# Splitting each raw weight tile into high and low parts in one operation per engine

## The chip, the cores and the metric

The kernel runs on one core of a Trainium2 chip. The metric is the device time in microseconds (us) of one execution, given as the median of several runs. The engines are TensorE (PE in the profile; its weight loads are listed as PEld), VectorE (DVE), ScalarE (ACT), GpSimd (POOL) and SyncE (SP), whose queue issues nearly all DMAs.

## The reference, cut to what matters

A decoder trunk of two layers in float32, with 256 tokens and 2048 channels. Nearly all of its arithmetic is products of the activations with weight matrices, and every one of these products that the change touches is computed to float32 accuracy.

```
# layer 0 (state space)
h  = modulate(rmsnorm(x, norm_g[0]), shift, scale)    # from c @ mod_w[0]
u, z = split(h @ w_in)                                # 2048 x 4096
y  = gelu(s5_scan(u))                                 # recurrence over tokens
y  = y * sigmoid(y @ w_glu + b_glu)
x  = x + gate * ((y * silu(z)) @ w_out)
# shared keys and values
kv = modulate(rmsnorm(x, kv_norm_g), ...) @ w_kv      # 2048 x 3072
# layer 1 (attention with three branches)
q, gates, z = split(h @ w_qg)                         # 2048 x (2048 + 48 + 6144)
o  = sum over branches of gates * silu(z) * attention(branch)
x  = x + gate * (o @ w_o)
return rmsnorm(x, final_norm_g)
```

The vectors shift, scale and gate come from products of one row, silu(c), with the matrices mod_w (2048 x 6144 for each layer) and kv_mod_w (2048 x 4096). All weights are read once.

## The kernel before

Activations lie with channels on the 128 partitions, as 16 blocks of [128, 256 tokens]. A weight matrix is cut into columns of 128, and each such column into two raw tiles of [128, 8, 128] float32, 512 KB each, which is 1024 columns on a partition. TensorE multiplies float32 numbers fast if they are first rounded to a shorter form (fp32r). So each weight tile and each activation is split: the high part is the rounded value, the low part is what is left. A product is then the sum of three: high x high, high x low, low x high (lines 227 to 229).

Raw tiles land in `ring`, a pool of 8 slots that all weights share: the split weights, those of the adaLN products that TensorE computes as they lie (`pe_mod_pair`, lines 155 and 157), and those that VectorE multiplies and sums (`dve_mod`, lines 142 and 144). One DMA on SP's queue fills one slot, and it is issued when what used the slot before has finished.

`split_w` (lines 194 to 205) cuts a raw tile of eight blocks into two halves of four blocks, 512 columns. For each half ScalarE writes the high part (line 202) and then VectorE subtracts it from the raw tile (line 203). The results lie in `hring`, a pool with 4 buffers of [128, 4, 128] for high parts and 4 for low parts. `project_half` (lines 222 to 229) consumes one raw tile with 24 matmuls: for each of eight blocks high x high, high x low, low x high. A high buffer is free after the last matmul of line 228 that reads it, a low buffer after the last of line 229.

The stages, in order of the profile: the adaLN products of layer 0 together with eight blocks of u, row by row of w_in (`u_rows`), to some 150 us; the tables of the state space layer and its scan, a recurrence of small VectorE operations (lines 608 to 611), with the blocks of u and z as filling, to some 410 us; the products with w_glu and w_out, to some 610 us; keys and values, compression and queries (four blocks of these row by row, `q_rows`, with raw tiles of 512 columns), to some 900 us; attention head by head with the 48 blocks of its z, to some 1260 us; the product with w_o and the last norm. A list written out by hand (`PLAN`) says at which point of the program the filling work stands: halves of u and z, adaLN products of TensorE and of VectorE, pieces of the compression and rows of the queries. The order of the instructions of each engine is then set when the program is built: the framework orders them by a timeline that it simulates, with the buffers that the pools have (`schedule_with_timeline_sim=True`). On the chip each engine and each DMA queue works in that order.

Of the kernel before, what the change touches and what calls it, by code (L numbers as in the profile page):

```python
# [37 lines left out]
# columns of the adaLN products, by blocks of 128: 0..47 layer 0, 48..95 layer 1, 96..127 keys and values.  # L38
# Blocks 0..31 come first; of the rest TensorE takes some (weights as they lie) and VectorE the others (turned round).
# [16 lines left out]
SK = 2  # L56
# what fills each slot of the program: u, z halves of blocks, m, d modulation (TensorE, VectorE),
# c pieces of the compression, q rows of the queries
# [12 lines left out]
def trunk_kernel(ctx, tc, xT, crow, ccol, vec, m0n, mn, mt, w_ur, w_in, w_glu, w_out, w_kv, w_qr, w_q, w_g,  # L71
# [3 lines left out]
    ring = ctx.enter_context(tc.tile_pool(name="ring", bufs=8))  # L75
    hring = ctx.enter_context(tc.tile_pool(name="hring", bufs=4))
# [16 lines left out]
    def raw_tile(name="raw"):  # L93
        return ring.tile([128, 8, 128], F32, tag="raw", name=name)

    # ---------------------------------------------------------------- constants
# [78 lines left out]
    # columns of modv: 0..47 layer 0, 48..95 layer 1, 96..127 kv  # L175
    def mod_finish(col, n):
        """Those of the columns col .. col + n that VectorE has summed, in two parts."""
        t = [x for x in range(col, col + n) if x in DVE_MODS]
        if t:
            c = slice(t[0], t[-1] + 1)  # L180
            assert len(t) == t[-1] + 1 - t[0]
            nc.vector.tensor_add(modv[:, c], modv[:, c], modw[:, c.start - 48:c.stop - 48])
            nc.vector.tensor_add(modv[:, c], modv[:, c], vv_("mb", c.start, c.stop))

    # ---------------------------------------------------------------- projections
# [8 lines left out]
    def split_w(r, n):  # L194
        """The first n of the eight blocks in r, four by four."""
        out = []
        for h in range(0, n, 4):
            c = min(4, n - h)
            hi = hring.tile([128, 4, 128], F32R, tag="hi", name="hi")
            lo = hring.tile([128, 4, 128], F32R, tag="lo", name="lo")  # L200
            rr = r[:, h:h + c, :]
            nc.scalar.activation(hi[:, 0:c, :], rr, AF.Copy)  # L202
            nc.vector.tensor_sub(lo[:, 0:c, :], rr, hi[:, 0:c, :].bitcast(F32))  # L203
            out.append((hi, lo))
        return out

    class Act:
        """A matrix [2048 channels, 256 tokens] as a high and a low part."""
# [13 lines left out]
    def project_half(src, act, half, acc):  # L222
        w = load_w(src, (half,))
        for k in range(8 * half, 8 * half + 8):
            hi, lo = w[(k - 8 * half) // 4]
            kk = k % 4
# [4 lines left out]
    def project(src, act):  # L231
        """The sums [128 columns, 256 tokens]."""
# [13 lines left out]
    def rms_scale(tot):  # L246
        """1 / sqrt(mean square over channels), for every token, on all partitions."""
# [7 lines left out]
    def norm_mod(xt, rstd, scol, bcol, act, ks=range(KT)):  # L255
        """act = split of (x * rstd) * S + B."""
# [7 lines left out]
    # ---------------------------------------------------------------- layer 0: modulation and u  # L264
    # (the first NR blocks of u, row by row of w_in as the modulation of the rows comes in)
# [14 lines left out]
    def u_rows(k):  # L280
# [6 lines left out]
        for i in range(NR):  # L287
            hi, lo = w[i // 4]
            acc = uacc[i // 2][:, i % 2, :]
            nc.tensor.matmul(acc, hi[:, i % 4, :], h0(0, k), start=(k == 0 and i % 2 == 0), stop=False,  # L290
                             skip_group_check=True)
            nc.tensor.matmul(acc, hi[:, i % 4, :], h0(1, k), start=False, stop=False, skip_group_check=True)
            nc.tensor.matmul(acc, lo[:, i % 4, :], h0(0, k), start=False, stop=(k == KT - 1),
# [10 lines left out]
    # ---------------------------------------------------------------- S5 tables  # L304
# [10 lines left out]
    def exact_exp(dst, src):  # L315
        """e^src to float32's accuracy: 2^k times a polynomial of what is left."""
# [40 lines left out]
    # powers a^1..a^4: [128, 64, 4] real, imaginary  # L357
# [20 lines left out]
    # coef  # L378
# [6 lines left out]
    # coef * a^(3-j): [128, 64, 4]  # L385
# [13 lines left out]
    # a^4 for the chunk recurrence  # L399
# [41 lines left out]
    for s in (2, 3, 0, 1):  # L441
# [11 lines left out]
        # C a^0 .. C a^3 side by side  # L453
# [5 lines left out]
        # K_d[c_in, c_out] = Re(C a^d Bbar) of the pairs (h = (l, q), b) at partitions (q, b, c_in)  # L459
# [16 lines left out]
        # the input tables turned round, in place: (b, j, c) on partitions, [h, r, g2, n]  # L476
# [30 lines left out]
    def u_turn(f):  # L507
        """Half of u, (g, e, c) on partitions, to (e, j, c) on partitions."""
# [53 lines left out]
    def scan_in(f):  # L562
        """Inputs of the recurrence over chunks."""
# [38 lines left out]
    def scan_run(f):  # L602
        """The recurrence over chunks."""
# [9 lines left out]
    def scan_local(f, tz):  # L613
        """What comes out of a chunk from its own inputs, in place of U."""
# [14 lines left out]
    def scan_out(f, cts):  # L629
        """The part of y that the states carry, on to U."""  # L630
        VH = VV[f]
        ys = VH[:, 0:8].rearrange("p h r b k -> p (h r b k)").rearrange("p (b g k) -> p b g k", g=4, k=64)
        for q in range(2):
# [10 lines left out]
            for g2 in range(2):  # L644
# [3 lines left out]
                else:  # L648
                    # VectorE is at the recurrence of the other half
# [53 lines left out]
    # ---------------------------------------------------------------- GLU  # L703
# [30 lines left out]
    # ---------------------------------------------------------------- shared keys and values  # L734
# [46 lines left out]
    def cmp_piece(e, i):  # L781
        """A quarter of the first product of a compression, then the rest of it."""
# [6 lines left out]
        for l in range(8 * half, 8 * half + 8):  # L789
            hi, lo = w[l // 4 - 2 * half]  # L790
            first, last = (h == 0 and l == 0), (h == 1 and l == 15)
            nc.tensor.matmul(cp, hi[:, l % 4, :], f[:, 0, l, :], start=first, stop=False)
            nc.tensor.matmul(cp, hi[:, l % 4, :], f[:, 1, l, :], start=False, stop=False)
            nc.tensor.matmul(cp, lo[:, l % 4, :], f[:, 0, l, :], start=False, stop=last)
# [44 lines left out]
    # (queries of the first heads, row by row of their weights as the modulation of the rows comes in)  # L839
# [3 lines left out]
    def q_rows():  # L843
# [21 lines left out]
        for i in range(QN):  # L865
            hi, lo = w[i // 4]
            acc = qacc[i // 2][:, i % 2, :]
            nc.tensor.matmul(acc, hi[:, i % 4, :], hq[0](0, k), start=(k == 0 and i % 2 == 0), stop=False,
# [254 lines left out]
```

## Time and profile before

| | |
|---|---|
| median of 3 runs | 1364.43 us (1359.98 to 1368.99) |
| span of the profiled execution | 1368.1 us |
| TensorE matmul busy | 1267.0 us, 93% |
| VectorE busy | 1068.3 us, 78% |
| ScalarE busy | 681.7 us, 50% |
| read from HBM | 326.10 MB, 242 GB/s over the span |
| split operations on full raw tiles of 1024 columns, two each | 640 on ScalarE, 640 on VectorE |

The profile is one execution, taken by the hardware profiler; its times stand against its own span, which lies 3.7 us above the median of the runs. An engine's busy time is the time in which one of its instructions ran; a duration reaches to the end of an instruction's writes, so that the next one of the same engine can start a little before it. A wait names the engine that waited, and what released it. In a list of DMAs the last number is the time from issue to landing.

### The profile page before, as it was taken

How to read it: one execution, taken by the hardware profiler on the slowest of the kernel's cores; microseconds unless marked ns; L12 is line 12 of the kernel's file. 1: busy time of each engine (PE TensorE's matmuls, PEld its weight loads, DVE VectorE, ACT ScalarE, POOL GpSimd, SP SyncE). 2: the span in 40 equal slices, each digit the busy share in tenths (PEclk: the TensorE clock that was granted, in tenths of full speed). 3: DMA queues.
4: the chain of work that ended last, by engine and by line, in shares of the span. 5: the costliest groups of instructions: out<-in, count | busy, mean ns of one | idle time of the engine just before them, and what ended most of it. 6: DMA issues, size and time to landing. Idle time of an engine off the chain costs nothing.

```text
span 1368.1 us, 31424 instructions
## 1 busy us (share of the span) xinstructions
PE 1267.0 (93%) x12270; PEld 1200.6 (88%) x12270; DVE 1068.3 (78%) x2612; ACT 681.7 (50%) x1439; POOL 42.5 (3%) x71
## 2 busy tenths in 40 slices
PE   2799979989999999997998999999999999999995
PEld 2678779878888999986997999999999999999995
DVE  5998318999997898889877878776878777777665
ACT  3345544423356555544453545555555555555653
POOL 1000500001001000000000000000000000000001
PEclk9999989999999999997899999999999999999998
DMA  9799966649788999985887888876555444444541
GB/s 359 275 347 336 316 200 200 205 172 336 242 300 299 321 357 318 327 305 187 293 303 248 277 295 289 274 253 227 170 193 194 165 144 141 159 142 161 186 155 62
DMA packets 94055, 332.88 MB, mean 243 GB/s; under 512 B 12785, under 2 KB 13025, under 8 KB 92881
## 3 DMA queue, kind: packets, MB, share of 16 engines
q1 hardware_dynamic: 91792, 321.45, 68.3%
q0 software_dynamic: 2112, 9.42, 2.1%
q8 instruction: 96, 1.57, 0.5%
q14 instruction: 55, 0.44, 0.1%
HBM read 326.10 MB, written 4.72 MB: 242 GB/s over the span
## 4 chain that ended last, share of the span: by engine, by line
PE 68%; DVE 15%; DMA 12%; issue 3%; ACT 2%; SPq 0%; DVEq 0%; ACTq 0%
PE acc L229 18%; PE acc L227 18%; PE acc L228 18%; DMA raw<-in_mt_dram 6%; DVE lo L203 3%; DMA raw<-in_w_in_dram 3%; DVE raw L144 2%; PE macc L157 2%; PE s L957 1%; DVE stab L608 1%; DMA mraw<-in_m0n_dram 1%; PE op L1008 1%; DVE stab L610 1%; PE kp L467 1%; DVE stab L609 1%
## 5 line engine op out<-in xcount | busy, mean ns | idle before, releaser
L202 ACT ACTIVATE hi<-raw 128x512 fp32r<-128x512 f32 x640 | 400.9, 631 | 466.1 <-PE acc L228 395.9
L203 DVE TENSOR_TENSOR lo<-raw,hi 128x512 fp32r<-128x512 f32 x640 | 435.0, 690 | 146.8 <-ACT hi L202 143.6
L228 PE MATMUL acc<-hq,hi 128*128 128x256 f32 x960 | 274.9, 286 | 0.0
L229 PE MATMUL acc<-hq,lo 128*128 128x256 f32 x960 | 271.5, 284 | 2.5 <-DVE lo L203 2.3
L227 PE MATMUL acc<-hq,hi 128*128 128x256 f32 x960 | 273.2, 285 | 0.4 <-ACT hi L202 0.4
L144 DVE SCALAR_TENSOR_TENSOR raw<-raw,cact 128x1024 f32<-128x1024 f32 x156 | 190.1, 1220 | 57.0 <-DMA raw<-in_mt_dram 56.6
L229 PEld LDWEIGHTS acc<-hq,lo 128*128 128x128 f32 x960 | 180.5, 189 | 5.4 <-DVE lo L203 3.9
L228 PEld LDWEIGHTS acc<-hq,hi 128*128 128x128 f32 x960 | 180.9, 188 | 3.7 <-issue 3.3
L227 PEld LDWEIGHTS acc<-hq,hi 128*128 128x128 f32 x960 | 180.9, 188 | 1.3 <-issue 0.7
L229 PE MATMUL acc<-h,lo 128*128 128x256 f32 x384 | 114.0, 297 | 12.7 <-DVE lo L203 12.3
L229 PE MATMUL acc<-hkv,lo 128*128 128x256 f32 x384 | 114.2, 299 | 5.1 <-DVE lo L203 4.6
L227 PE MATMUL acc<-hkv,hi 128*128 128x256 f32 x384 | 112.5, 295 | 4.9 <-ACT hkv L260 4.9
L227 PE MATMUL acc<-h,hi 128*128 128x256 f32 x384 | 113.5, 296 | 1.0 <-ACT hi L202 1.0
L228 PE MATMUL acc<-hkv,hi 128*128 128x256 f32 x384 | 111.9, 294 | 0.8 <-DVE hkv L261 0.8
L228 PE MATMUL acc<-h,hi 128*128 128x256 f32 x384 | 111.6, 291 | 0.0
L229 PEld LDWEIGHTS acc<-h,lo 128*128 128x128 f32 x384 | 76.1, 198 | 17.4 <-DVE lo L203 14.0
L229 PEld LDWEIGHTS acc<-hkv,lo 128*128 128x128 f32 x384 | 77.3, 202 | 7.6 <-DVE lo L203 7.2
L227 PEld LDWEIGHTS acc<-hkv,hi 128*128 128x128 f32 x384 | 77.3, 202 | 5.8 <-ACT hkv L260 5.8
L227 PEld LDWEIGHTS acc<-h,hi 128*128 128x128 f32 x384 | 76.1, 198 | 5.3 <-issue 2.5
L228 PEld LDWEIGHTS acc<-hkv,hi 128*128 128x128 f32 x384 | 77.4, 202 | 1.4 <-DVE hkv L261 1.4
L157 PE MATMUL macc<-mraw,cz 128*32 128x128 f32 x1600 | 59.0, 300 | 18.9 <-DMA mraw<-in_m0n_dram 17.9
L228 PEld LDWEIGHTS acc<-h,hi 128*128 128x128 f32 x384 | 76.1, 198 | 0.1
(312 smaller groups left out, 2829.6 us busy)
## 6 DMA issues: line engine op xcount, KB each, us to landing
raw<-in_mt_dram SPq DMA_DIRECT2D x156, 512.0 KB, 5.6
raw<-in_w_z_dram SPq DMA_DIRECT2D x96, 512.0 KB, 3.7
mraw<-in_m0n_dram SPq DMA_DIRECT2D x64, 512.0 KB, 7.8
raw<-in_w_in_dram SPq DMA_DIRECT2D x48, 512.0 KB, 6.1
raw<-in_w_kv_dram SPq DMA_DIRECT2D x48, 512.0 KB, 5.2
mraw<-in_mn_dram SPq DMA_DIRECT2D x36, 512.0 KB, 6.6
raw<-in_w_glu_dram SPq DMA_DIRECT2D x32, 512.0 KB, 6.3
raw<-in_w_out_dram SPq DMA_DIRECT2D x32, 512.0 KB, 6.1
```

The source lines that it names most:

```text
L144: nc.vector.scalar_tensor_tensor(out=rf, in0=rf, scalar=1.0, in1=cact[:, 1024 * e:1024 * e + 1024], op0=OP.mult, op1=OP.mult, accum_out=mo ...
L157: nc.tensor.matmul(acc[32 * j:32 * j + 32, 128 * e:128 * e + 128], cz[:, q, :], r[:, q % 8, :], start=(e == 0 and q < 4), stop=(q >= 12), ...
L202: nc.scalar.activation(hi[:, 0:c, :], rr, AF.Copy)
L203: nc.vector.tensor_sub(lo[:, 0:c, :], rr, hi[:, 0:c, :].bitcast(F32))
L227: nc.tensor.matmul(acc, hi[:, kk, :], act(0, k), start=(k == 0), stop=False)
L228: nc.tensor.matmul(acc, hi[:, kk, :], act(1, k), start=False, stop=False)
L229: nc.tensor.matmul(acc, lo[:, kk, :], act(0, k), start=False, stop=(k == KT - 1))
L467: nc.tensor.matmul(kp[32 * q:32 * q + 32, l, :], bb[r][pr, 32 * h:32 * h + 32], kc_[pr, 2 * h:2 * h + 2, r, :], start=(l == 0 and r == 0), ...
L608: V.tensor_mul(ra, VH[:, :, :, :, k], ar)
L609: V.tensor_mul(rb, VH[:, :, ::-1, :, k], ai)
L610: V.tensor_add(ra, ra, VH[:, :, :, :, k + 1])
L957: nc.tensor.matmul(sp, qo(a, h)[:, qs], kk[:, kv, b, o:o + w], start=(i == 0), stop=(i == 2))
```

## The change

A raw tile is split as a whole: one operation of ScalarE and one of VectorE on 1024 columns. The tiles of `hring` become [128, 8, 128], twice as large, and there are 3 of each kind instead of 4. The ring of raw tiles has 6 slots instead of 8. In bytes of a partition, the two pools together hold what they held: 8 x 4 KB + 8 x 2 KB before, 6 x 4 KB + 6 x 4 KB after. The consumers take their block from the one large tile, and the gate weights are split in two steps instead of four. The diff also takes comments out, which is left out here, as are two other consumers that change in the same way (`cmp_piece`, `q_rows`).

```diff
-    ring = ctx.enter_context(tc.tile_pool(name="ring", bufs=8))
-    hring = ctx.enter_context(tc.tile_pool(name="hring", bufs=4))
+    ring = ctx.enter_context(tc.tile_pool(name="ring", bufs=6))
+    hring = ctx.enter_context(tc.tile_pool(name="hring", bufs=3))
...
     def split_w(r, n):
-        """The first n of the eight blocks in r, four by four."""
-        out = []
-        for h in range(0, n, 4):
-            c = min(4, n - h)
-            hi = hring.tile([128, 4, 128], F32R, tag="hi", name="hi")
-            lo = hring.tile([128, 4, 128], F32R, tag="lo", name="lo")
-            rr = r[:, h:h + c, :]
-            nc.scalar.activation(hi[:, 0:c, :], rr, AF.Copy)
-            nc.vector.tensor_sub(lo[:, 0:c, :], rr, hi[:, 0:c, :].bitcast(F32))
-            out.append((hi, lo))
-        return out
+
+        hi = hring.tile([128, 8, 128], F32R, tag="hi", name="hi")
+        lo = hring.tile([128, 8, 128], F32R, tag="lo", name="lo")
+        rr = r[:, 0:n, :]
+        nc.scalar.activation(hi[:, 0:n, :], rr, AF.Copy)
+        nc.vector.tensor_sub(lo[:, 0:n, :], rr, hi[:, 0:n, :].bitcast(F32))
+        return [(hi, lo)]
...
     def project_half(src, act, half, acc):
         w = load_w(src, (half,))
         for k in range(8 * half, 8 * half + 8):
-            hi, lo = w[(k - 8 * half) // 4]
-            kk = k % 4
+            hi, lo = w[0]
+            kk = k % 8
...
         for i in range(NR):
-            hi, lo = w[i // 4]
+            hi, lo = w[i // 8]
...
-    for h in range(4):
-        ghi = hring.tile([128, 4, 128], F32R, tag="hi", name="ghi")
-        glo = hring.tile([128, 4, 128], F32R, tag="lo", name="glo")
-        if h % 2 == 0:
-            gr = raw_tile("gr")
-            nc.sync.dma_start(gr[:, :, 0:48], w_g[:, 4 * h:4 * h + 8, :])
-        rr = gr[:, 4 * (h % 2):4 * (h % 2) + 4, 0:48]
+    for h in range(2):
+        ghi = hring.tile([128, 8, 128], F32R, tag="hi", name="ghi")
+        glo = hring.tile([128, 8, 128], F32R, tag="lo", name="glo")
+        gr = raw_tile("gr")
+        nc.sync.dma_start(gr[:, :, 0:48], w_g[:, 8 * h:8 * h + 8, :])
+        rr = gr[:, :, 0:48]
```

## Rows read from the trace of the kernel before

**Rows 1.** The head of the page: the span of the profiled execution.
```profile
span 1368.1 us, 31424 instructions
```

**Rows 2.** Busy time by stretch; first the stretch, its length, then the columns named.
```profile
core 0: us, PE busy (x) PEld busy (x) DVE busy (x) ACT busy (x) POOL busy (x), PEclk, DMA share, GB/s
0.00:171.00 171.00, 133.61 (x1904) 111.83 (x1904) 126.14 (x283) 75.92 (x175) 26.93 (x49) 0.96 0.93 327
...
205.00:410.00 205.00, 190.89 (x2558) 172.02 (x2557) 191.28 (x638) 85.51 (x160) 7.27 (x6) 0.95 0.71 242
410.00:600.00 190.00, 187.99 (x1550) 183.72 (x1549) 162.45 (x314) 106.09 (x192) 4.22 (x13) 1.00 0.91 323
600.00:925.00 325.00, 298.60 (x2329) 288.68 (x2327) 262.78 (x538) 160.15 (x319) 0.00 (x0) 0.94 0.79 270
925.00:1334.00 409.00, 409.00 (x3319) 399.71 (x3319) 300.73 (x796) 229.36 (x552) 0.00 (x0) 1.00 0.50 169
```

**Rows 3.** Groups by line: count | busy us, mean ns of one | idle before.
```profile
L203 DVE TENSOR_TENSOR lo<-raw,hi 128x512 fp32r<-128x512 f32 x640 | 435.0, 690 | 146.8 <-ACT hi L202 143.6
```

**Rows 4.** Waits over the span: who waited <- for whom: us, times, longest.
```profile
ACT hi L202 <- PE acc L228: 402.2, 449, 5.3
...
DVE raw L144 <- DMA raw<-in_mt_dram: 56.6, 41, 3.6
...
PE acc L229 <- DVE lo L203: 20.5, 19, 4.3
```

**Rows 5.** Waits for low parts, 205 to 410 us, then 600 to 925 us.
```profile
PE acc L229 <- DVE lo L203: 12.3, 5, 4.3
...
PE acc L229 <- DVE lo L203: 6.9, 11, 1.4
```

**Rows 6.** Timeline of VectorE, 60 to 92 us: start, duration, instruction.
```profile
63.89 1.22 DVE L432 TENSOR_TENSOR tmB<-bc,stab 128x1024 f32<-128x1024 f32 x1
65.03 0.48 DVE L259 SCALAR_TENSOR_TENSOR xn<-x,scol,rstd 128x256 f32<-128x256 f32 x1
...
69.22 1.29 DVE L203 TENSOR_TENSOR lo<-uraw,hi 128x512 fp32r<-128x512 f32 x2
70.43 0.15 DVE L277 SCALAR_TENSOR_TENSOR scol<-modv,vecs 128x1 f32<-128x1 f32 x1
```

**Rows 7.** Line 203 by stretch: length, its busy time on VectorE (count).
```profile
205.00:410.00 205.00, 55.60 (x81) 0.95 0.71 242
...
600.00:925.00 325.00, 124.46 (x186) 0.94 0.79 270
925.00:1334.00 409.00, 164.98 (x243) 1.00 0.50 169
```

**Rows 8.** Timeline of ScalarE, high parts alone, at 151 us and from 212 us.
```profile
151.09 1.15 ACT L202 ACTIVATE hi<-uraw 128x512 fp32r<-128x512 f32 x2 [0.51 <-DMA uraw<-in_w_ur_dram]
...
212.01 0.63 ACT L202 ACTIVATE hi<-raw 128x512 fp32r<-128x512 f32 x1 [0.79 <-PE acc L228]
213.43 0.63 ACT L202 ACTIVATE hi<-raw 128x512 fp32r<-128x512 f32 x1 [0.79 <-PE acc L228]
```

**Rows 9.** Groups by line: ScalarE's widest copy.
```profile
L455 ACT ACTIVATE tmB<-ctA 128x1536 f32<-128x1536 f32 x4 | 5.9, 1486 | 6.3 <-DVE ctA L439 6.3
```

**Rows 10.** Waits of SP's queue over the span.
```profile
SPq L190 <- DVE lo L203: 275.3, 119, 4.9
```

**Rows 11.** The page's DMA issues: count, KB each, median us to landing.
```profile
raw<-in_w_z_dram SPq DMA_DIRECT2D x96, 512.0 KB, 3.7
mraw<-in_m0n_dram SPq DMA_DIRECT2D x64, 512.0 KB, 7.8
...
raw<-in_w_out_dram SPq DMA_DIRECT2D x32, 512.0 KB, 6.1
```

**Rows 12.** Line 190, 410 to 600 us: its waiters (none), then its busy slices.
```profile
who waited for it (us, times):
busy tenths in 40 slices 0000000000000000000000000000000000000000
```

More of the change, by code (lines that the diff above doesn't have):

```diff
@@ L287, in u_rows @@
         for i in range(NR):
-            hi, lo = w[i // 4]
+            hi, lo = w[i // 8]
             acc = uacc[i // 2][:, i % 2, :]
-            nc.tensor.matmul(acc, hi[:, i % 4, :], h0(0, k), start=(k == 0 and i % 2 == 0), stop=False,
+            nc.tensor.matmul(acc, hi[:, i % 8, :], h0(0, k), start=(k == 0 and i % 2 == 0), stop=False,
                              skip_group_check=True)
-            nc.tensor.matmul(acc, hi[:, i % 4, :], h0(1, k), start=False, stop=False, skip_group_check=True)
-            nc.tensor.matmul(acc, lo[:, i % 4, :], h0(0, k), start=False, stop=(k == KT - 1),
+            nc.tensor.matmul(acc, hi[:, i % 8, :], h0(1, k), start=False, stop=False, skip_group_check=True)
+            nc.tensor.matmul(acc, lo[:, i % 8, :], h0(0, k), start=False, stop=(k == KT - 1),
                              skip_group_check=True)
@@ L789, in cmp_piece @@
         for l in range(8 * half, 8 * half + 8):
-            hi, lo = w[l // 4 - 2 * half]
+            hi, lo = w[0]
             first, last = (h == 0 and l == 0), (h == 1 and l == 15)
-            nc.tensor.matmul(cp, hi[:, l % 4, :], f[:, 0, l, :], start=first, stop=False)
-            nc.tensor.matmul(cp, hi[:, l % 4, :], f[:, 1, l, :], start=False, stop=False)
-            nc.tensor.matmul(cp, lo[:, l % 4, :], f[:, 0, l, :], start=False, stop=last)
+            nc.tensor.matmul(cp, hi[:, l % 8, :], f[:, 0, l, :], start=first, stop=False)
+            nc.tensor.matmul(cp, hi[:, l % 8, :], f[:, 1, l, :], start=False, stop=False)
+            nc.tensor.matmul(cp, lo[:, l % 8, :], f[:, 0, l, :], start=False, stop=last)
         if i < 3:
@@ L865, in q_rows @@
         for i in range(QN):
-            hi, lo = w[i // 4]
+            hi, lo = w[i // 8]
             acc = qacc[i // 2][:, i % 2, :]
-            nc.tensor.matmul(acc, hi[:, i % 4, :], hq[0](0, k), start=(k == 0 and i % 2 == 0), stop=False,
+            nc.tensor.matmul(acc, hi[:, i % 8, :], hq[0](0, k), start=(k == 0 and i % 2 == 0), stop=False,
                              skip_group_check=True)
-            nc.tensor.matmul(acc, hi[:, i % 4, :], hq[0](1, k), start=False, stop=False, skip_group_check=True)
-            nc.tensor.matmul(acc, lo[:, i % 4, :], hq[0](0, k), start=False, stop=(k == KT - 1),
+            nc.tensor.matmul(acc, hi[:, i % 8, :], hq[0](1, k), start=False, stop=False, skip_group_check=True)
+            nc.tensor.matmul(acc, lo[:, i % 8, :], hq[0](0, k), start=False, stop=(k == KT - 1),
                              skip_group_check=True)
@@ L910, in trunk_kernel @@
     acc = ps.tile([128, L], F32, tag="mm", name="acc")
-    for h in range(4):
-        ghi = hring.tile([128, 4, 128], F32R, tag="hi", name="ghi")
-        glo = hring.tile([128, 4, 128], F32R, tag="lo", name="glo")
-        if h % 2 == 0:
-            gr = raw_tile("gr")
-            nc.sync.dma_start(gr[:, :, 0:48], w_g[:, 4 * h:4 * h + 8, :])
-        rr = gr[:, 4 * (h % 2):4 * (h % 2) + 4, 0:48]
+    for h in range(2):
[4 more added lines that the diff above has]
+        rr = gr[:, :, 0:48]
         nc.scalar.activation(ghi[:, :, 0:48], rr, AF.Copy)
         V.tensor_sub(glo[:, :, 0:48], rr, ghi[:, :, 0:48].bitcast(F32))
-        for k in range(4):
-            kt = 4 * h + k
+        for k in range(8):
+            kt = 8 * h + k
             nc.tensor.matmul(acc[0:48, :], ghi[:, k, 0:48], hq(0, kt), start=(kt == 0), stop=False)
```

## The prediction

> **What bounds the kernel now.** I read the stretches first: busy time of each engine, granted clock and DMA share in five parts of the span [rows 1, 2]. From 925 to 1334 us TensorE is busy 409.00 of 409.00 us, and from 410 to 600 us 188 of 190, at full clock: there nothing that VectorE or ScalarE saves can come out. From 205 to 410 us VectorE is busy 191.3 of 205 us (93%), beside a TensorE at 93% whose matmuls partly run at less than full clock (0.95). From 600 to 925 us TensorE idles 26.4 of 325 us. Up to 171 us the DMA engines are busy 93%, at 327 GB/s. So the change can gain in some 530 us of the span, lose in all of it, and its operations are tied to two supplies, the ring of raw tiles and the split tiles.
>
> The group of the low-part operation gives its size [rows 3]: 640 of 128x512, 690 ns each. The view of waits then says who is held up [rows 4]. ScalarE's high-part operation stood 402.2 us waiting for matmuls that read the high tile: the split tiles are full and paced by TensorE, which is how a saturated consumer looks. VectorE's adaLN product waited 56.6 us for its tile to land. TensorE itself waited for a low part only 19 times, 20.5 us in all. Of these, 12.3 us (5 times) lie in 205 to 410 us and 6.9 us (11 times) in 600 to 925 us [rows 5].
>
> **VectorE, what is saved.** Durations overlap a little between neighbours, so I count from start to start [rows 6]. Two low parts start at 69.22 us and the next operation at 70.43: 1.21 us a raw tile now. The 128x1024 product of two SBUF tensors starts at 63.89 us and its follower at 65.03: 1.14 us, which I take for the new operation (same engine, same width, all float32). That is 0.07 us a tile, not the 0.16 us by which two durations exceed one (2 x 690 - 1220 ns). In 205 to 410 us there are 81 low parts, some 40 tiles: 40 x 0.07 = 2.8 us [rows 7]. In 600 to 925 us there are 186, so 93 tiles and 6.5 us; VectorE is busy 81% there and TensorE 92%, so I count a third, 2 us. The 243 from 925 us on [rows 7] save VectorE 8.5 us that nobody needs: a full TensorE hides them, and so from 410 to 600 us. Total on the path: -5 us; bounds 0 and -9.3.
>
> **ScalarE.** Two high parts in a row take 1.15 us, one alone 0.63 [rows 8]. The new one is not in the trace; a 128x1536 copy takes 1.49 us [rows 9], so between 0.63 and 1.49, by the straight line 0.63 + 512 x (1.49 - 0.63) / 1024 = 1.06 us. ScalarE is busy 106 of 190 us at most, so the sum takes nothing for it.
>
> **Latency and the split tiles.** From the start of the high part to the end of the first low part it is now 0.63 + 0.69 = 1.32 us; after, 1.06 + 1.22 = 2.28 us, 0.96 more. The third buffer stands against this. TensorE uses up half a raw tile in 1.42 us (the high parts follow at that pace, 212.01 and 213.43 us [rows 8]), so when a buffer comes free it now has three halves in hand, 4.3 us, against a refill of 1.3: margin 3.0 us. After, it has two whole tiles, 5.7 us, against 2.3: margin 3.4 us. The margins are nearly equal, so I expect about as many late low parts, each later. Bounds: if all 19 waits grow by 0.96 us, +18 us; if the wider margin ends them all, -20.5 us. I take +4: the five in 205 to 410 us grow by the longer operation alone (1.22 - 0.69 = 0.53 us, 2.6 us), and of the eleven in 600 to 925 us a few outlast the wider margin.
>
> The weight queries of 512 columns and the gate keep their work; the gate's two raw tiles are split in 2 operations an engine instead of 4, at most 0.2 us. TensorE's instructions are the same in number and size; nothing is counted for them.
>
> **The ring, eight to six.** The DMA issues on SP's queue stand behind one another, and the raw weights alone waited 275.3 us (119 times) for VectorE to release a slot [rows 10]: the ring is full. So I share out a slot's time. In 410 to 600 us, 323 GB/s is 0.616 tiles of 524,288 B a us; eight slots at that rate are held 13.0 us each, and landing takes 6.1 (w_out) [rows 11], so 6.9 us are left for waiting and use. Six slots are held 9.7 us: 3.6 us left, while a split needs 2.28 and an adaLN product 1.22. In 600 to 925 us (270 GB/s, 0.515 a us) it is 15.5 us against 11.7. In the first stretch (0.624 a us) 12.8 against 9.6, with 7.8 us of landing. But that landing is mostly a queue: a tile in the quiet last stretch lands in 3.7 us. Two tiles fewer ahead in the queue take off 2 / 0.624 = 3.2 us and leave the DMA engines as busy. The slack lies with the weights: from 410 to 600 us no instruction at all waited for one of them to land [rows 12]. They park in the ring until a split tile is free, and the third split tile takes one of them out. So the ring's slack shrinks rather than runs out. Bounds: nothing, and +46 us (rival one). I take +4, nearer to nothing, because the shares above still hold.
>
> **Sum.** -5 + 4 + 4 = +3 us on the profile's own 1368.1 us: about 1371. The median of the runs is 1364.43, 3.7 below the profiled execution, so the forecast for the median is 1367 us: no change that a measurement of this kernel can tell, which needs about 1%, 14 us. One thing is in no term: the program's planner sets each engine's order anew from the new sizes and buffer counts; it can go either way and is in the width.
>
> **Rivals.** One, slower: the ring starves VectorE's adaLN products. They come just in time already (56.6 us of waits, 41 times [rows 4]), and VectorE takes its work in order, so a late adaLN tile holds up the low parts behind it, and TensorE behind those. If holds and landings stay as they are, six slots and one more split tile do the work of seven in eight; 600 to 925 us stretch by 325 / 7 = 46 us at most. About half would show, since TensorE still has its 5.7 us in hand: 1364 + 3 + 23 = 1390. It decides once the 3.6 us left after landing fall under the 2.28 us of a split. For it speaks the full ring; against it that the weights, not the adaLN tiles, hold most of the slack. The Trainium skill (Perfetto Trace Analysis, Optimization Strategy) says that a gap that keeps coming back on the engine that should be saturated can mean too little room for the next tile; the trace of before shows no such gap from 925 us on.
>
> Two, slower: the longer operation itself makes TensorE wait. 19 waits x 0.96 = 18 us, less the 5 saved: 1364 + 13 = 1377, about 1% slower, and more where waits now hidden come up. For it: VectorE and ScalarE are not saturated over most of the span. Against it: the margin of 3.4 us. The Trainium skill (Perfetto Trace Analysis, Optimizing Scalar/DVE Operations) has both halves of this: grouping into larger operations helps a saturated engine, and where Scalar or Vector are not saturated but cause bubbles elsewhere, breaking instructions up lets work finish sooner. By its second half the change goes the wrong way outside 205 to 410 us.
>
> Three, faster: the deeper split buffer ends the waits for low parts (20.5 us) and VectorE's saving counts in full (9.3 us): up to -30 us. With two thirds of that, 1364 - 20 = 1344. For it: the third tile and VectorE's 93%. Against it: the margin grows by 0.4 us only.
>
> **Chances.** No change 0.46 (its own range 1352 to 1378), ring 0.20, latency 0.13, faster 0.21. Of the latency case the most lies just above 1%, so slower has 0.33, faster 0.21, within 1% 0.46. From 1346 to 1392 about 2 in 10 are left out, one at each end.
>
> **What would show it.** Right: 320 low parts on raw tiles instead of 640 at about 1.22 us; VectorE's busy time down by some 20 us or more; TensorE still full from the attention on; its waits for low parts between 10 and 40 us. The ring is the culprit if VectorE's waits for adaLN tiles rise far above 56.6 us and the DMA share of the busy stretches falls. The latency is, if TensorE's waits for low parts grow while those stay. The forecast is wrong on the gain side if TensorE's 26.4 us of idle time from 600 to 925 us mostly go.

## The result, and the profile after

The change made the kernel slower by 1.0%: 1376.82 us median of 8 runs (1371.57 to 1385.74) against 1365.11 us of 8 runs before on the same chip, ratio 1.0098 with a 95% interval of 1.0071 to 1.0125. The forecast was 1367 us and no change, in a range of 1346 to 1392. The measured time lies in the range, at the very edge of "within 1%", and on the slower side of it.

A caution for the traces: the span of the profiled execution of before (1368.1 us) lies 3.0 us above the median of its runs, that of after (1373.8 us) 3.0 us below. So the two traces show 5.7 us of the 11.7. The head of the page after:

```profile
span 1373.8 us, 30259 instructions
## 1 busy us (share of the span) xinstructions
PE 1265.2 (92%) x12270; PEld 1199.9 (87%) x12270; DVE 1034.8 (75%) x2274; ACT 621.6 (45%) x1101; POOL 40.4 (3%) x71
```

VectorE's busy time fell by 33.5 us and ScalarE's by 60, TensorE's stayed. The stretches that answer to [rows 2], with the same columns:

```profile
0.00:171.00 171.00, 126.61 (x1850) 109.28 (x1854) 124.02 (x263) 73.22 (x154) 23.58 (x46) 0.90 0.91 315
...
205.00:410.00 205.00, 191.18 (x2567) 173.16 (x2567) 186.10 (x588) 77.56 (x119) 7.06 (x6) 0.94 0.69 233
410.00:600.00 190.00, 190.00 (x1571) 185.13 (x1568) 162.70 (x258) 97.06 (x131) 3.78 (x13) 1.00 0.93 332
600.00:925.00 325.00, 291.99 (x2269) 282.47 (x2268) 249.07 (x431) 139.02 (x222) 0.00 (x0) 0.93 0.78 266
925.00:1334.00 409.00, 409.00 (x3318) 399.45 (x3318) 283.96 (x689) 208.38 (x436) 0.00 (x0) 1.00 0.51 171
```

Two stretches got worse: the first (327 to 315 GB/s, granted clock 0.96 to 0.90, fewer matmuls done) and the one from 600 us (TensorE 298.6 to 292.0 us, with 2269 matmul records instead of 2329). From 925 us on TensorE is as full as it was. The groups and the waits that answer to [rows 3, 4]:

```profile
L199 ACT ACTIVATE hi<-raw 128x1024 fp32r<-128x1024 f32 x320 | 338.5, 1059 | 477.9 <-PE acc L224 321.4
L200 DVE TENSOR_TENSOR lo<-raw,hi 128x1024 fp32r<-128x1024 f32 x320 | 390.4, 1222 | 126.7 <-ACT hi L199 125.3
```

```profile
ACT hi L199 <- PE acc L224: 327.7, 183, 5.6
...
DVE raw L144 <- DMA raw<-in_mt_dram: 56.2, 39, 3.5
...
PE acc L225 <- DVE lo L200: 17.9, 15, 3.8
...
PE uacc L286 <- ACT hi L199: 8.9, 8, 1.8
...
PE acc L223 <- ACT hi L199: 7.1, 6, 3.2
```

VectorE's waits for adaLN tiles did not move (56.6 to 56.2 us). TensorE's waits for low parts fell a little (20.5 to 17.9), but its waits for high parts grew, from 2.4 to 8.9 us for the rows of u and from 1.9 to 7.1 us elsewhere. Those before:

```profile
PE uacc L290 <- ACT hi L202: 2.4, 2, 1.7
...
PE acc L227 <- ACT hi L202: 1.9, 4, 0.6
```

To see where the time went, cut the program by work instead of by the clock: the start of the last matmul that reads a low part for the rows of u (end of the first stage), for u and z (end of the scan stage), and for w_out (the operand is called ghl). Before, then after; the last two numbers ahead of the semicolon are the first and the last start in us:

```profile
L293 PE MATMUL uacc<-h,lo x128: 274/282/583, 43.5 to 157.4; 128*128 128x256 f32 x128
...
L229 PE MATMUL acc<-h,lo x384: 274/281/583, 158.5 to 426.1; 128*128 128x256 f32 x192
...
L229 PE MATMUL acc<-ghl,lo x256: 278/281/376, 521.3 to 612.2; 128*128 128x256 f32 x128
```

```profile
L289 PE MATMUL uacc<-h,lo x128: 274/282/583, 43.7 to 165.6; 128*128 128x256 f32 x128
...
L225 PE MATMUL acc<-h,lo x384: 274/281/579, 166.7 to 427.1; 128*128 128x256 f32 x192
...
L225 PE MATMUL acc<-ghl,lo x256: 279/281/285, 519.6 to 610.4; 128*128 128x256 f32 x128
```

The first stage ends 8.2 us later (157.4 to 165.6). The scan stage wins 7.2 of that back (268.7 to 261.5 us), the next one 2.8 (186.1 to 183.3). Then comes the query stage: keys, values, compression and the row-wise queries, from the last matmul on ghl to the last that fills the row-wise queries. One line for before and one for after, columns as [rows 2]:

```profile
612.43:847.55 235.12, 211.64 (x1622) 204.31 (x1622) 191.69 (x386) 111.56 (x219) 0.00 (x0) 0.92 0.79 268
```

```profile
610.60:856.70 246.10, 214.26 (x1621) 205.57 (x1621) 189.55 (x332) 100.10 (x161) 0.00 (x0) 0.91 0.77 261
```

It is 11.0 us longer for the same matmuls (1622 and 1621 records): 8.4 us more of idle TensorE (23.5 to 31.8) and 2.6 us more busy time, at a granted clock of 0.91 instead of 0.92. What follows, the last query blocks, the attention and the product with w_o, took 3.4 us less. So there are two losses, the first stage and the query stage, and smaller gains between and behind them.

### The profile page after: what moved, and what is told of

Its sections match the earlier page's. It is cut to its first block, busy times and chain, and to the rows that moved or that the text cites. A ratio compares the mean times of both kernels' runs of the same rounds, so it can differ in the third digit from the quotient of the medians.

```text
span 1373.8 us, 30259 instructions
## 1 busy us (share of the span) xinstructions
PE 1265.2 (92%) x12270; PEld 1199.9 (87%) x12270; DVE 1034.8 (75%) x2274; ACT 621.6 (45%) x1101; POOL 40.4 (3%) x71
## 4 chain that ended last, share of the span: by engine, by line
PE 69%; DMA 13%; DVE 12%; issue 3%; ACT 2%; SPq 0%; DVEq 0%; ACTq 0%
PE acc L223 18%; PE acc L225 18%; PE acc L224 18%; DMA raw<-in_mt_dram 6%; DVE lo L200 3%; DMA raw<-in_w_in_dram 2%; DMA mraw<-in_m0n_dram 2%; DVE raw L144 2%; DMA uraw<-in_w_ur_dram 2%; PE macc L157 2%; PE s L952 1%; ACT hi L199 1%; DVE stab L604 1%; PE yp L637 1%; PE op L1003 1%
## 5 line engine op out<-in xcount | busy, mean ns | idle before, releaser
L199 ACT ACTIVATE hi<-raw 128x1024 fp32r<-128x1024 f32 x320 | 338.5, 1059 | 477.9 <-PE acc L224 321.4
L200 DVE TENSOR_TENSOR lo<-raw,hi 128x1024 fp32r<-128x1024 f32 x320 | 390.4, 1222 | 126.7 <-ACT hi L199 125.3
L144 DVE SCALAR_TENSOR_TENSOR raw<-raw,cact 128x1024 f32<-128x1024 f32 x156 | 189.4, 1220 | 57.2 <-DMA raw<-in_mt_dram 56.2
L223 PE MATMUL acc<-hkv,hi 128*128 128x256 f32 x384 | 114.6, 300 | 8.4 <-ACT hkv L256 4.4
L224 PE MATMUL acc<-hkv,hi 128*128 128x256 f32 x384 | 113.1, 296 | 1.4 <-DVE hkv L257 1.4
```

What stands on the lines that cost most here:

```text
L144: nc.vector.scalar_tensor_tensor(out=rf, in0=rf, scalar=1.0, in1=cact[:, 1024 * e:1024 * e + 1024], op0=OP.mult, op1=OP.mult, accum_out=mo ...
L199: nc.scalar.activation(hi[:, 0:n, :], rr, AF.Copy)
L200: nc.vector.tensor_sub(lo[:, 0:n, :], rr, hi[:, 0:n, :].bitcast(F32))
L223: nc.tensor.matmul(acc, hi[:, kk, :], act(0, k), start=(k == 0), stop=False)
L224: nc.tensor.matmul(acc, hi[:, kk, :], act(1, k), start=False, stop=False)
```

## Experiments: taking the change apart

The change does four things at once: six raw slots instead of eight, more room for split tiles, split tiles that are filled and freed as a whole, and one operation instead of two. The first four runs undo or do these one by one. Ratios are against the kernel before on the same chip, with 95% intervals.

**Only the ring.** The kernel before with six slots.

```diff
-    ring = ctx.enter_context(tc.tile_pool(name="ring", bufs=8))
+    ring = ctx.enter_context(tc.tile_pool(name="ring", bufs=6))
```

> The kernel before with the ring of raw tiles cut from 8 slots to 6 and nothing else: halves of 512 columns, 4 split buffers of half a tile. Ring theory (the lost slots make the first, DMA-bound stretch and the query stretch later): at least what the change cost, 1377 us or more, up to 1390, because no third split tile takes a weight out of the ring; the last matmul of the rows of u at 164 us or later (157.7 before, 165.9 after the change). Latency theory (the operation on 1024 columns is what costs): 1363 to 1369 us, as before. Planner theory (any new order of the instructions costs or gains some us, whatever the cause): no telling, within 15 us of before.

Measured: 1391.37 us, ratio 1.018 (1.0152 to 1.0208). The ring alone costs 25 us, more than the change, and a little more than expected. The first stage ends 5.5 us late, and the query stage is as long as after the change (VectorE's waits for adaLN tiles, last line, are over the whole span):

```profile
L293 PE MATMUL uacc<-h,lo x128: 274/281/422, 43.0 to 162.9; 128*128 128x256 f32 x128
```

```profile
626.70:873.20 246.50, 217.00 (x1622) 209.00 (x1623) 194.16 (x389) 111.42 (x219) 0.00 (x0) 0.90 0.77 256
```

```profile
DVE raw L144 <- DMA raw<-in_mt_dram: 70.0, 58, 3.6
```

**The changed kernel's buffers, the old operations and halves.**

```diff
-    ring = ctx.enter_context(tc.tile_pool(name="ring", bufs=8))
-    hring = ctx.enter_context(tc.tile_pool(name="hring", bufs=4))
+    ring = ctx.enter_context(tc.tile_pool(name="ring", bufs=6))
+    hring = ctx.enter_context(tc.tile_pool(name="hring", bufs=6))
```

> The changed kernel's buffers with the old operations: a ring of 6, and split buffers of 24 KB a partition as 6 of half a tile each, split in two operations of 512 columns. Ring theory: as the changed kernel, 1372 to 1380 us, with the rows of u ending near 165 us. Latency theory: 1363 to 1368 us. If release by halves is what the old kernel gained from, between the two, about 1370.

Measured: 1367.79 us, ratio 1.0013 (0.9991 to 1.0035): the move of 8 KB from the ring to the split tiles costs nothing that can be told, if the halves stay. The time lies in the range of the latency theory, the end of the rows of u (165.5 us) where the ring theory had it. The trace shows a loss and a gain of the same size. The rows of u end late, as with every ring of six, the scan stage is 9.4 us longer (278.1 us), and w_out ends 14.4 us later than before. The query stage is 14.9 us shorter than before, and TensorE's waits for low parts are a third:

```profile
L293 PE MATMUL uacc<-h,lo x128: 274/281/576, 42.7 to 165.5; 128*128 128x256 f32 x128
...
L229 PE MATMUL acc<-ghl,lo x256: 279/281/285, 535.9 to 626.6; 128*128 128x256 f32 x128
```

```profile
626.90:847.10 220.20, 203.72 (x1624) 198.88 (x1624) 191.80 (x389) 110.18 (x219) 0.00 (x0) 0.95 0.85 288
```

```profile
PE acc L229 <- DVE lo L203: 7.0, 4, 4.5
```

**The new tiles, filled by the old operations.** Ring 6 and three whole split tiles as changed, two operations per engine into each.

```diff
-        rr = r[:, 0:n, :]
-        nc.scalar.activation(hi[:, 0:n, :], rr, AF.Copy)
-        nc.vector.tensor_sub(lo[:, 0:n, :], rr, hi[:, 0:n, :].bitcast(F32))
+        for h in range(0, n, 4):
+            rr = r[:, h:h + 4, :]
+            nc.scalar.activation(hi[:, h:h + 4, :], rr, AF.Copy)
+            nc.vector.tensor_sub(lo[:, h:h + 4, :], rr, hi[:, h:h + 4, :].bitcast(F32))
```

> The changed kernel with each whole split tile filled by two operations of 512 columns per engine instead of one of 1024; ring 6 and 3 split tiles as changed. It isolates the size of the operation. Ring theory: as the changed kernel, 1373 to 1380 us. Latency theory: back to 1364 to 1368 us. VectorE's saving gone: its busy time some 30 us higher than with the change, with at most 3 us on the time.

Measured: 1372.03 us, ratio 1.0047 (1.0026 to 1.0068). Between the two: the whole tiles cost 0.34% beside halves in the same memory (1.0013 to 1.0047), the whole operations another 0.51% (to 1.0098). The first step is hardly larger than the uncertainty of the two ratios that it lies between (about 0.30% taken together), the second is one and a half times as large as its own (about 0.34%); their sum, 0.85%, is well clear of it. In the trace the first step is a loss and a gain: the scan stage is 9.4 us shorter than with halves (268.7 us), and the query stage, 232.7 us here, is 12.5 us longer than with halves and 13.4 shorter than with whole operations:

```profile
617.30:850.00 232.70, 208.15 (x1611) 201.00 (x1611) 189.62 (x384) 104.94 (x215) 0.00 (x0) 0.93 0.78 267
```

**The new operations with the old ring.**

```diff
-    ring = ctx.enter_context(tc.tile_pool(name="ring", bufs=6))
-    hring = ctx.enter_context(tc.tile_pool(name="hring", bufs=3))
+    ring = ctx.enter_context(tc.tile_pool(name="ring", bufs=8))
+    hring = ctx.enter_context(tc.tile_pool(name="hring", bufs=2))
```

> The new operations with the old ring: splits of 1024 columns, 8 raw slots, 2 split tiles of 1024 columns of each kind (16 KB, as before). Ring theory: the first stretch as before (rows of u end near 158 us) and 1364 to 1370 us in all, unless two split tiles are too few. Latency theory: slower than the changed kernel, 1380 to 1420 us, since with two tiles only one is in hand (2.85 us) while the next takes 2.28 us to split, and TensorE's waits for low parts rise over 50 us.

Measured: 1506.07 us, ratio 1.1021 (1.0997 to 1.1044), worse than any theory had put it. The first stage is as early as before, which the ring of eight gives back, but two whole tiles are far too few: TensorE waits 90 us for low parts, five times as long as after the change.

```profile
L289 PE MATMUL uacc<-h,lo x128: 274/282/583, 44.6 to 155.3; 128*128 128x256 f32 x128
```

```profile
PE acc L225 <- DVE lo L200: 90.0, 53, 5.1
```

So two whole tiles of each kind lose far more than the ring of eight gives back, and in this memory three of each kind leave six slots. That is why the change had to take its slots from the ring.

## Experiments: which operation, which order, how much is scatter

**One engine whole, the other in halves.** Two runs on the changed kernel; the first leaves ScalarE's operation whole, the second VectorE's.

```diff
-        nc.vector.tensor_sub(lo[:, 0:n, :], rr, hi[:, 0:n, :].bitcast(F32))
+        for h in range(0, n, 4):
+            nc.vector.tensor_sub(lo[:, h:h + 4, :], r[:, h:h + 4, :], hi[:, h:h + 4, :].bitcast(F32))
```

> The changed kernel with ScalarE's high part in one operation of 1024 columns and VectorE's low part in two of 512. Of the 1376.8 us after the change, and the 1372.0 with both engines at 512, it tells whose longer operation costs. If ScalarE's (the first matmul of a tile and the first low part wait 0.43 us longer for it): 1375 to 1378 us. If VectorE's (TensorE's first low-part matmul waits 0.53 us longer): 1371 to 1373 us. In the latency theory the two add up, so this one and the next should together exceed 1372.0 by the 4.8 us.

```diff
-        nc.scalar.activation(hi[:, 0:n, :], rr, AF.Copy)
+        for h in range(0, n, 4):
+            nc.scalar.activation(hi[:, h:h + 4, :], r[:, h:h + 4, :], AF.Copy)
```

> The counterpart: two high parts of 512 columns on ScalarE, one low part of 1024 on VectorE, which then has to wait for both high parts. VectorE's saving is kept (0.07 us a tile, some 7 us of the scan stage by the profile after the change), ScalarE's is not. Latency theory: 1373 to 1377 us, the kv and query stage (from the last matmul on ghl to the last of the row-wise queries) between 233 us (both at 512) and 246 us (both at 1024). Without a latency effect: 1366 to 1370 us, since VectorE's saving alone is left.

Measured: 1385.77 us, ratio 1.0125 (1.0093 to 1.0156), and 1386.75 us, ratio 1.0127 (1.0095 to 1.016). Neither came as expected: both should have lain between the run with all halves (1.0047) and the change (1.0098), and both lie above. The query stage alone agrees with a cost of either whole operation, 241 and 245 us, next to 232.7 with none and 246.1 with both:

```profile
624.40:865.60 241.20, 210.35 (x1610) 203.03 (x1611) 190.26 (x383) 99.03 (x159) 0.00 (x0) 0.92 0.77 258
```

```profile
622.90:868.20 245.30, 211.84 (x1622) 202.33 (x1623) 188.92 (x330) 105.24 (x216) 0.00 (x0) 0.93 0.77 262
```

The rest of their excess lies mostly in the scan stage (276.0 and 272.1 us, against 268.7 with all halves and 261.5 after the change) and stays unexplained. Whose operation costs more is not told by these runs.

**How much a new order alone moves.** The planner lays out the instructions anew for each kernel. Two controls change only the order of the fillers in the first slot of the list, once in the kernel before and once in the changed one.

```diff
-    "zzm", "", "um", "u", "d", "z", "z", "d", "m", "z", "zu", "zz", "dm", "m", "zm", "zmz", "z", "mz", "zzzz",
+    "mzz", "", "um", "u", "d", "z", "z", "d", "m", "z", "zu", "zz", "dm", "m", "zm", "zmz", "z", "mz", "zzzz",
```

> The kernel before with nothing changed but the order of the fillers in the first slot of the hand-written list (an adaLN product of TensorE before two halves of z, instead of behind them). No buffer and no operation changes; the planner lays out a part of the instructions anew. It sizes what a new order alone is worth. If differences of 5 us mean something: within 3 us of before, 1363 to 1369 us. If the planner's order alone scatters the time (planner theory): 5 us or more away, and the steps of 4 to 5 us between the other runs cannot be told from it.

> The changed kernel with only the fillers of the first slot in the other order, as was done with the kernel before (where it made 0.2% of difference). The size of the planner's own scatter on this side. If a new order is worth little: 1373 to 1380 us, and the changed kernel's 11 us are its own. If the order scatters the time by 8 us or more here: the runs with one engine's operation whole and the other's in halves, which came out slower than both neighbours, are scatter too, and so may be the step of 4.8 us from halves to whole operations.

Measured: 1366.3 us, ratio 0.9977 (0.9953 to 1.0001), and 1381.21 us, ratio 1.0101 (1.0085 to 1.0116). The second lies 1.2 us above the range for a new order of little worth. On either side the order moves the ratio by at most 0.23%, and the changed kernel is 1.0% slower in both orders. So, as far as two orders tell, the 1.0% is the change's own; the query stage too is longer in both (235.1 and 232.0 us before, 246.1 and 244.8 after). Two orders are a small sample; the steps of 0.34% and 0.51% above, and the 0.3% by which the two mixed runs exceed the change, are not far over this scatter.

**The low parts read last.** Is the late low part the cause? Then let TensorE work on the high part first: all 16 matmuls on it, then the 8 on the low part.

```diff
+        hi, lo = w[0]
         for k in range(8 * half, 8 * half + 8):
-            hi, lo = w[0]
             kk = k % 8
             nc.tensor.matmul(acc, hi[:, kk, :], act(0, k), start=(k == 0), stop=False)
             nc.tensor.matmul(acc, hi[:, kk, :], act(1, k), start=False, stop=False)
-            nc.tensor.matmul(acc, lo[:, kk, :], act(0, k), start=False, stop=(k == KT - 1))
+        for k in range(8 * half, 8 * half + 8):
+            nc.tensor.matmul(acc, lo[:, k % 8, :], act(0, k), start=False, stop=(k == KT - 1))
```

> The changed kernel with the matmuls of a raw tile in another order: all 16 that read the high part, then the 8 that read the low part. TensorE then has 1.9 us of work on a tile before it needs its low part, which is more than the 1.22 us of the operation. Latency theory: TensorE's waits for low parts (17.9 us after the change) fall under 5 us, and the time to 1364 to 1370 us. If those waits are only where a lateness shows that DMA or VectorE's load makes anyway: another wait (for the high part) takes their place, 1374 to 1380 us. The high tile is freed earlier and the low tile later than now in the run of a tile, which should not matter with three.

Measured: 1363.67 us, ratio 0.9964 (0.9937 to 0.9991): faster than before by a little, and 1.3% faster than the change. The waits for low parts went from 17.9 us in 15 waits to 9.9 in 2, not under 5 us as expected, and the query stage from 246.1 to 226.0 us:

```profile
PE acc L226 <- DVE lo L200: 9.9, 2, 7.9
```

```profile
613.40:839.40 226.00, 203.79 (x1620) 198.14 (x1621) 187.84 (x328) 101.11 (x161) 0.00 (x0) 0.95 0.81 280
```

This would have spoken for the latency theory, were it not for the counter-run: the same order in the kernel before, by halves.

```diff
-        for k in range(8 * half, 8 * half + 8):
-            hi, lo = w[(k - 8 * half) // 4]
-            kk = k % 4
-            nc.tensor.matmul(acc, hi[:, kk, :], act(0, k), start=(k == 0), stop=False)
-            nc.tensor.matmul(acc, hi[:, kk, :], act(1, k), start=False, stop=False)
-            nc.tensor.matmul(acc, lo[:, kk, :], act(0, k), start=False, stop=(k == KT - 1))
+        for q, (hi, lo) in enumerate(w):
+            ks = range(8 * half + 4 * q, 8 * half + 4 * q + 4)
+            for k in ks:
+                nc.tensor.matmul(acc, hi[:, k % 4, :], act(0, k), start=(k == 0), stop=False)
+                nc.tensor.matmul(acc, hi[:, k % 4, :], act(1, k), start=False, stop=False)
+            for k in ks:
+                nc.tensor.matmul(acc, lo[:, k % 4, :], act(0, k), start=False, stop=(k == KT - 1))
```

> The kernel before with its matmuls in the other order within each half tile (eight on the high part, then four on the low part); ring 8 and 4 half split buffers as before. It tells whether that order is worth something by itself or only undoes what the change costs. If it only undoes the latency of the longer operation: within 3 us of before, 1362 to 1369 us. If waits for low parts cost the old kernel too (20.5 us of them): 1350 to 1360 us.

Measured: 1349.12 us, ratio 0.9867 (0.9848 to 0.9886). This is the fastest kernel of the study and beats both. The order is worth 1.3% by itself, with or without the change, and a little more than expected. It did not earn this by ending the waits for low parts, as the expectation had it: they are as long as before (21.1 us against 20.5). Its query stage is 219.9 us instead of 235.1: 5.4 us less idle time of TensorE and 9.9 us less busy time (for 1613 matmul records instead of 1622), at a granted clock of 0.96 instead of 0.92. What did fall there are VectorE's waits for adaLN tiles, 33.7 us before (third line) and 20.1 with this order (last line):

```profile
PE acc L230 <- DVE lo L203: 21.1, 18, 3.9
```

```profile
609.52:829.43 219.91, 201.79 (x1613) 195.38 (x1613) 189.68 (x385) 111.34 (x219) 0.00 (x0) 0.96 0.83 286
```

```profile
DVE raw L144 <- DMA raw<-in_mt_dram: 33.7, 19, 3.6
```

```profile
DVE raw L144 <- DMA raw<-in_mt_dram: 20.1, 13, 3.6
```

**The same order with the changed kernel's buffers, in halves.** The ring of 6 and six half split buffers, as in the second run, with the diff of the last.

> The same order of the matmuls with the changed kernel's share of the buffers: ring 6, 6 half split buffers, operations of 512 columns. Against the whole tiles with that order (1363.7 us) it shows what the larger operation and tile cost once the low part is no longer waited for. Latency theory: nothing is left of it, 1360 to 1367 us. If the size costs through something else (VectorE's order, release by whole tiles): 1352 to 1358 us.

Measured: 1362.17 us, ratio 0.9964 (0.9946 to 0.9982), the same ratio as the whole tiles with that order. So with the high parts read first, whole tiles and operations cost nothing in sum beside halves in the same buffers: their query stage is 12.8 us longer (226.0 against 213.2) and their scan stage 10.5 us shorter (267.0 against 277.5). And the move of 8 KB from the ring to the split tiles costs 1.0% (0.9867 to 0.9964), which in the old order cost 0.13%. The trace shows where: the loss before the query stage stays, w_out ending at 626.1 us, while the query stage, short already, gains only 6.7 us more (219.9 to 213.2):

```profile
L230 PE MATMUL acc<-ghl,lo x256: 279/281/285, 536.0 to 626.1; 128*128 128x256 f32 x128
```

```profile
626.40:839.60 213.20, 200.55 (x1612) 197.15 (x1613) 188.44 (x384) 108.05 (x214) 0.00 (x0) 0.94 0.84 292
```

**One low tile for one raw slot.** Whole tiles, high parts first, a ring of 7, three high and two low tiles. The diff shows the buffers alone; the order of the matmuls is that of the first run with the low parts read last.

```diff
-    ring = ctx.enter_context(tc.tile_pool(name="ring", bufs=6))
+    ring = ctx.enter_context(tc.tile_pool(name="ring", bufs=7))
...
-        lo = hring.tile([128, 8, 128], F32R, tag="lo", name="lo")
+        lo = hring.tile([128, 8, 128], F32R, tag="lo", name="lo", bufs=2)
```

> Whole tiles and the order high parts first, with one low buffer (4 KB a partition) given back to the ring: 7 raw slots, 3 high and 2 low split tiles. The low part is then read only in the last third of a tile's run. If the ring of 6 still costs (rows of u ended 5 to 8 us late with it): 1355 to 1361 us. If two low tiles are too few, as two of both kinds were: 1375 us or more.

Measured: 1378.18 us, ratio 1.0078 (1.0052 to 1.0104). With seven slots the first stage is as early as with eight (156.8 us), which puts its loss on the step from seven to six. But VectorE now stood 68.6 us waiting for a low tile to be read and freed, against 25.7 us in the same order with three low tiles, and the whole is 1.1% slower than that run (1.0078 against 0.9964): the low tile was worth more than the slot:

```profile
L290 PE MATMUL uacc<-h,lo x128: 274/281/583, 44.2 to 156.8; 128*128 128x256 f32 x128
```

```profile
DVE lo L200 <- PE acc L226: 68.6, 84, 1.7
```

## Why the prediction was right or wrong

**The number.** The middle of the forecast was 10 us too fast. That it was no further off is partly luck: where I had put +4 and +4 for the ring and the latency, the first stage holds +8.2 and the query stage +11.0 us, and -7.2, -2.8 and -3.4 in the others hide most of it. Rival two had named 1377 us, which is what was measured, but by another mechanism: TensorE's waits for low parts were to grow by 18 us, and they fell by 2.6. And every sign that I had named for "right" came (320 low parts at 1.22 us, 33.5 us less of VectorE, a full TensorE from the attention on, 17.9 us of waits), with a kernel that is 1.0% slower: the signs could not tell the cases apart.

**VectorE's saving.** The durations came as taken: 1059 ns for the high part (1.06 by the straight line) and 1222 ns for the low part (1.22). From start to start the low part takes 1.14 us, as the nearest row had it:

```profile
66.79 1.23 DVE L200 TENSOR_TENSOR lo<-uraw,hi 128x1024 fp32r<-128x1024 f32 x1
67.93 1.22 DVE L435 TENSOR_TENSOR ctA<-tmB 128x1024 f32<-128x1024 f32 x1
```

The scan stage, where VectorE is busiest, became 7.2 us shorter, 268.7 to 261.5 us; with the new tiles filled by halves it took 268.7. I had put 2.8 there. That does not show the saving: the changed kernel with the other filler order takes 267.7 us (270.9 before in that order), and the run that kept VectorE's operation whole and gave ScalarE halves takes 272.1. The stage also starts 8.2 us later, so part of the 7.2 may be work that only moved. What the term is worth on the path is not settled. That a full TensorE hides all savings from 925 us on was right: 409.00 of 409.00 us.

**The ring.** The term of +4 us was mis-sized, most plainly in the first stretch. I argued that the first stretch's landing was mostly a queue and two tiles fewer would be free. Every kernel with six slots ended the rows of u at 162.8 to 166.1 us (with the other filler order at about 168), every one shown with seven or eight at 155.3 to 157.4. That is 5 to 9 us, the 8.2 of the change among them. Nor was the slack as safe as "shrinks rather than runs out" had it. From 410 to 600 us, where nobody waited for a weight before [rows 12], ScalarE now waited 15.3 us:

```profile
who waited for it (us, times):
  ACT hi L199: 15.3, 11
```

TensorE was still full there (190.00 of 190). With six slots and the old split tiles it was not so well covered: the products with w_glu and w_out took 192.1 us instead of 186.1. The rival named for the ring had the wrong victim: VectorE's waits for adaLN tiles did not rise (56.2 us). They do rise with the ring of six alone, to 70.0 us, and fall to 37.8 with the larger split buffer in halves, so the extra split tiles make up for the slots there. With the change the weights and the first stage paid, not the adaLN products: ScalarE's waits for w_in to land went from 25.8 to 49.4 us, those for the rows of u from 5.9 to 19.1.

**Latency and the split tiles.** This is the term that was furthest off. I compared two margins, 3.0 and 3.4 us, and called them equal. The comparison that mattered was with the same memory in halves: five half tiles in hand when one comes free, 5 x 1.42 = 7.1 us against a refill of 1.3, a margin of 5.8. With it the waits for low parts fall to 7.0 us and the query stage is 26 us shorter than after the change (220.2 against 246.1). So the change had an 8 KB larger split buffer that could have paid for the ring, and whole tiles and whole operations took that away. The +4 I put on latency can't be set against the +11.0 us of the query stage alone, where the terms meet: there the ring of six costs 11.4 us (246.5), the larger split buffer in halves gives back 26.3 (220.2), and whole tiles with whole operations cost 25.9 (246.1).

I had also looked at the wrong wait. Over the span TensorE waits less for low parts, but in the query stage VectorE waits twice as long for ScalarE's high part (10.7 us before, 22.7 after; 27.1 after with the other filler order, 14.3 in the new tiles filled by halves). TensorE's own waits there went from 4.6 to 8.8 us for low parts and from 1.3 to 5.6 for high parts (3.9 of it on the line shown), and one wait of 3.1 us is for the low part of the gate, where I had counted at most 0.2 us. Before, then after, in the query stage:

```profile
DVE lo L203 <- ACT hi L202: 10.7, 16, 1.9
...
PE acc L229 <- DVE lo L203: 4.6, 8, 1.4
```

```profile
DVE lo L200 <- ACT hi L199: 22.7, 18, 3.3
...
PE acc L225 <- DVE lo L200: 8.8, 9, 2.8
...
PE acc L223 <- ACT hi L199: 3.9, 5, 1.1
...
PE acc L919 <- DVE glo L914: 3.1, 1, 3.1
```

The Trainium skill (Perfetto Trace Analysis, Optimizing Scalar/DVE Operations) says that where Scalar or Vector are not saturated but cause bubbles on other engines, breaking up instructions may let work finish sooner. In the query stage the trace agrees: VectorE is busy 189.6 of 246.1 us, and in the old order of the matmuls the kernels with a ring of six, three whole tiles and one or two whole operations need 241 to 246 us there, the same tiles filled by halves 232.7.

**The sum.** It had -5, +4 and +4. By the traces: first stage +8.2, scan stage -7.2, the next -2.8, query stage +11.0, the rest -3.4 and -0.1 at the end, together +5.7 of the 11.7 us between the medians. The other 6 us are between one profiled execution and the median of its kind on either side.

**What stays open.** Why reading the high parts first is worth 1.3%: its own reason, fewer waits for low parts, is refuted for the kernel before. What goes with it in the query stage is that high buffers come free earlier (after 16 of a tile's 24 matmuls instead of 23, in halves after 8 of 12 instead of 11): ScalarE's waits for them fall from 66.0 to 45.2 us in the kernel before and from 64.5 to 23.7 in the changed one, VectorE's waits for adaLN tiles from 33.7 to 20.1 and from 31.3 to 14.0. That the one causes the other was not isolated. Why one whole operation with one in halves is slower than either pure form. And, as the changed order alone recovers the change's whole cost while it is worth as much to the old kernel, the late low part can't be called the shown cause of the 1.0%. What is shown is the balance: six slots cost 1.8% alone, the memory given to split tiles returns nearly all of it when used in halves, and about half as much when used in whole tiles with whole operations.

## What to carry to other kernels

Two operations made into one save only what lies between their starts (here 1.21 to 1.14 us), and when the buffer behind them becomes one tile, it is twice as coarse: count what the consumer has in hand when a buffer comes free, and compare with the same memory in small pieces, not only with the kernel as it was. Slots taken from a prefetch ring were felt here where DMA is the bound, in the first stage, and again in the query stage, so price them stage by stage. And run the counter-experiment: a cure that helps the old kernel as much as the new one says nothing of what the change broke.

## What the runs showed of the hardware

Stalls of TensorE went with more than their own length. In the query stage the same matmuls (1610 to 1624 records in the lines shown) took 200.6 to 217.0 us of busy time, and the lines with more idle TensorE tend to be those with more busy time and a lower granted clock: 12.6 to 18.1 us idle go with 200.6 to 203.7 us busy at 0.94 to 0.96, 29.5 to 33.5 us idle with 210.4 to 217.0 us at 0.90 to 0.93. From 12.6 to 29.5 us of idle time the busy time grows by 16.4 us, about as much as the idle time. This is a comparison of runs; no run changes the stalls alone.
